# Embedding stage of a hybrid decoder step: row factor applied in the gate's tanh, norm weights folded into the gate's weights, the affine step folded into the products, and the last tile's input projection issued ahead

## The chip, the core and the metric

The kernel runs on one core of a Trainium2 chip. The core has five engines that run side by side and wait for each other by semaphores: TensorE (PE in the profile, with its weight loads as PEld), VectorE (DVE), ScalarE (ACT), GpSimd (POOL) and SyncE (SP). Each engine works through its own instructions in the order that was fixed when the kernel was built. Transfers are issued from the queues of SP, ACT and POOL and carried by 16 DMA engines. The metric is the time of one execution on the device, in microseconds (us). Times of the same kernel in several runs are given by their median.

## What is computed

One layer of a decoder: RMSNorm and token mixing (retention and RWKV-7), a mixture of experts with product keys (PEER), then the per-layer input embedding that the change is about, and a final RMSNorm. There are 1024 prompt tokens and 64 sample tokens, the model is 1024 wide, and an input row has 256 elements. Cut to the end of the layer:

```python
def rmsnorm(x, g):
    y = x * lax.rsqrt(jnp.mean(x * x, axis=-1, keepdims=True) + RMS_EPS)
    return y * g
...
    h = h + peer(rmsnorm(h, norm_ffn), peer_wq, peer_keys, peer_u, peer_v)
    gate = jax.nn.sigmoid(rmsnorm(h, ple_norm) @ ple_gate)
    h = h + gate * (p_l @ ple_proj)
...
    y = rmsnorm(h, norm_final)
```

The row factor of a norm is 1/sqrt(mean + eps), one number for each token. `g`, here `ple_norm`, is one number for each of the 1024 columns.

## The kernel before

**Tokens and tiles.** The 1088 tokens are nine tiles: 0 to 7 with 128 prompt tokens each, and tile 8 with the 64 sample tokens. The mixture of experts is computed in two ways. For tiles 0 and 1 (`E0`) and tiles 8, 2 and 3 (`G1`) the chosen rows of the two expert tables are gathered: `gather` fetches, for each of a token's 128 experts, one row of 4 KB per token by an indirect DMA on POOL's queue (L1157, 128 rows of 4 KB in one fetch, into one of five buffers named `grow`). VectorE makes the dot product with it (L1171, first table) or adds it, weighted, to the running sum `gacc` (L1185, second table). For tiles 4 to 7 (`G2`) all 16384 experts are computed with matmuls: `dense_fused` and `dense_stored` call `dense`, which loads a piece of the second table (`vraw`, four buffers), splits it, and adds to `yT`.

**Splitting.** fp32 operands are split in a high and a low part (`split`, L304 to L308): ScalarE copies and rounds the high part, and VectorE (L306) or GpSimd (L308) subtracts it. `mm3` (L333 to L336) then makes three matmuls: high by high, high by low, low by high.

**The embedding stage's weights.** `ple_weights` runs as a side task within `dense_stored`, one step at every fourth piece of the table. Each step loads 128x512 of a weight into one of the `vraw` buffers (tile `pgr`, L1420) and splits it on ScalarE and GpSimd: 4 pieces for the projection (`pproj`), 16 for the gate (`pgate`). The parts lie in `pga`, `pgb` and `pgx`.

**The embedding stage.** `ple` (L1424 on) goes through the tiles in the order 0, 1, 4, 5, 6, 7, 8, 2, 3. It takes small tiles from one of two pools in turn, and `h` from three buffers. For each tile it

- loads the tile's input rows, transposed (`pt`, L1433), and splits them into `pth` and `ptl`, the low part on VectorE;
- loads h (L1438) and adds the experts' result: for tile 3, the last, the gather's sum straight from its PSUM home (L1440); for the other gathered tiles from DRAM (`py`, L1444, L1445); for tiles 4 to 7 transposed out of `yT` (`pyt`, L1450, L1451);
- calls `norm_T` (L310 on): Square with a sum on ScalarE (L314, `njunk`), the root on GpSimd in two instructions (`rsq`, L298, L299, `nrs`), then on VectorE h times row factor times `ple_norm` (L318, also into `njunk`), and `split_T`: eight transposes on TensorE (L327, `ntr`) and the split into `pxh` and `pxl`;
- for each half of 512 columns: 24 matmuls of the gate (`ppg`), tanh on ScalarE (L1460, `psg`), `0.5 t + 0.5` on VectorE (L1461, which makes the sigmoid), 6 matmuls of the input projection (`ppp`), product (L1464) and addition to h (L1465). `ppg` and `ppp` come from the same two PSUM buffers;
- for the final norm: Square (L1468, `fsq`), root (`frs`), two products (L1473, `fin`), and two stores from ACT's queue (L1474).

The gather of tile 3 is issued in the text ahead of `dense`, and it still runs while the first eight tiles go through `ple`. The last tile's h therefore waits for the last of its 128 sums.

**What sets the order.** The kernel is written with a framework that fixes each engine's order at build time: a list scheduler takes, on a modelled timeline, the ready instruction that stands first in the program text. It is switched on by `tile.TileContext(nc, schedule_with_timeline_sim=True)`. So an edit to one instruction can move others on every engine. Tiles of one pool with the same tag share buffers, and the next user of a buffer waits until the last reader is done.

## Time and profile before

| | us |
|---|---|
| runs shown: lowest, median, highest (3) | 3652.43, 3653.45, 3653.52 |
| profiled execution, its own time | 3657.16 |
| profiled execution, span from first to last instruction | 3655.2 |
| PE busy | 3242.7 (89%) |
| DVE busy | 2842.8 (78%) |
| POOL busy | 2343.4 (64%) |
| ACT busy | 1215.9 (33%) |

The profile is one execution on the chip, recorded by the hardware. A row of a *group* gives line, engine and operation, result and operands by their names in the program with their shapes, the count, the busy time and the mean duration in ns, and behind the second bar the idle time of that engine just before, with what ended most of it. A row of the *timeline* gives start, duration, engine, line, operation, and in brackets the idle time before. A row of a *window* table gives, for one stretch, its length, the busy time (and number of instructions) of each engine, the clock granted to TensorE as a share of full speed, the share of time in which the DMA engines were busy, and the GB/s that they moved. A row of *waits* gives who waited for whom, the sum, the number of times and the longest.

### The profile page before, as it was taken

To read this page: it belongs to the slowest core of one execution; us is meant where nothing else is said; L and a number is where in the kernel's file an instruction comes from. 1 tells how busy PE (TensorE), PEld (TensorE's weight loads), DVE (VectorE), ACT (ScalarE), POOL (GpSimd) and SP (SyncE) were. 2 spreads that over 40 slices of the span, in tenths; PEclk is the share of its full clock that TensorE was granted. 3 is DMA by queue.
4 is the path that set the end of the run, shared out by engine and by line. 5 is a ranking of instruction groups with operands and counts; after the bars stand their busy time and mean duration, and the time that the engine had idled before them with its cause. 6 is when DMAs were issued, how large, how long until landed. Compare 5 with 4: busy or idle time off the path is not lost. (4 is left out here: it accounts for less than half of the span.)

```text
span 3655.2 us, 51715 instructions
## 1 busy us (share of the span) xinstructions
PE 3242.7 (89%) x17493; PEld 2685.5 (73%) x17493; DVE 2842.8 (78%) x5663; ACT 1215.9 (33%) x2247; POOL 2343.4 (64%) x2076
## 2 busy tenths in 40 slices
PE   7797996887878888879999999899999999889995
PEld 7697996764756666758877887788888877667773
DVE  4544688888797787879977999777777777788887
ACT  4233121111211111222235888843333333333321
POOL 5352677554445555544489786578888878888743
PEclk9798997557978777889999999999999999999997
DMA  7267599779957888896589988899999999999975
GB/s 263 89 198 237 196 328 325 258 275 312 323 191 266 295 277 282 283 345 211 170 268 328 349 296 331 321 315 340 339 349 342 344 325 371 360 369 365 328 249 186
DMA packets 416995, 1059.97 MB, mean 290 GB/s; under 512 B 45467, under 2 KB 140953, under 8 KB 412058
## 3 DMA queue, kind: packets, MB, share of 16 engines
q0 software_dynamic: 165888, 604.05, 46.3%
q1 hardware_dynamic: 197902, 364.96, 30.1%
q10 hardware_dynamic: 52940, 87.64, 6.4%
q8 instruction: 139, 2.28, 0.2%
q14 instruction: 126, 1.03, 0.1%
HBM read 968.88 MB, written 87.56 MB: 289 GB/s over the span
## 5 line engine op out<-in xcount | busy, mean ns | idle before, releaser
L1157 POOL DMA_INDIRECT grow<-in_pv,eid x576 | 568.6, 987 | 500.7 <-DVE gacc L1185 244.9
L1157 POOL DMA_INDIRECT grow<-in_pu,eid x576 | 562.3, 976 | 355.3 <-DVE grow L1171 209.6
L1185 DVE SCALAR_TENSOR_TENSOR gacc<-grow,ac,gacc 128x1024 f32<-128x1024 f32 x571 | 731.6, 1281 | 49.7 <-DMA grow<-in_pv,eid 41.9
L1171 DVE SCALAR_TENSOR_TENSOR grow<-grow,gacc 128x1024 f32<-128x1024 f32 x576 | 689.5, 1213 | 83.0 <-DMA grow<-in_pu,eid 76.7
L1347 PE MATMUL py<-ah,vh 128*128 128x512 f32 x1024 | 405.0, 396 | 28.2 <-ACT vh L304 25.6
L333 PE MATMUL ph<-cx,uh 128*128 128x512 f32 x1024 | 404.1, 395 | 3.3 <-ACT uh L304 3.2
L1348 PE MATMUL py<-al,vh 128*128 128x512 f32 x1024 | 403.8, 394 | 0.5 <-DVE al L306 0.5
L334 PE MATMUL ph<-cx,uh 128*128 128x512 f32 x1024 | 402.2, 393 | 0.0
L308 POOL TENSOR_TENSOR vl<-vraw,vh 128x512 fp32r<-128x512 f32 (+2 forms) x232 | 327.5, 1416 | 31.1 <-ACT vh L304 19.9
L308 POOL TENSOR_TENSOR ul<-uraw,uh 128x1024 fp32r<-128x1024 f32 x128 | 308.2, 2408 | 50.4 <-ACT uh L304 30.3
L1350 PE MATMUL py<-ah,vl 128*128 128x512 f32 x1024 | 276.0, 398 | 16.2 <-POOL vl L308 15.7
L336 PE MATMUL ph<-cx,ul 128*128 128x512 f32 x1024 | 265.0, 395 | 3.9 <-POOL ul L308 3.9
L1347 PEld LDWEIGHTS py<-ah,vh 128*128 128x128 f32 x1024 | 194.3, 190 | 78.8 <-ACT vh L304 34.5
L304 ACT ACTIVATE vh<-vraw 128x512 fp32r<-128x512 f32 (+2 forms) x232 | 156.1, 675 | 280.0 <-PE py L1348 99.0
L1350 PEld LDWEIGHTS py<-ah,vl 128*128 128x128 f32 x1024 | 190.7, 189 | 70.8 <-POOL vl L308 30.8
L1354 DVE TENSOR_TENSOR yT<-yT,py 128x512 f32<-128x512 f32 x224 | 153.1, 684 | 109.0 <-PE py L1350 99.7
L1348 PEld LDWEIGHTS py<-al,vh 128*128 128x128 f32 x1024 | 194.5, 190 | 42.6 <-DVE al L306 1.9
L333 PEld LDWEIGHTS ph<-cx,uh 128*128 128x128 f32 x1024 | 192.8, 188 | 42.6 <-ACT uh L304 4.1
L336 PEld LDWEIGHTS ph<-cx,ul 128*128 128x128 f32 x1024 | 191.4, 189 | 43.4 <-POOL ul L308 5.4
L334 PEld LDWEIGHTS ph<-cx,uh 128*128 128x128 f32 x1024 | 193.0, 188 | 38.1
L304 ACT ACTIVATE uh<-uraw 128x1024 fp32r<-128x1024 f32 x128 | 135.5, 1059 | 169.9 <-DMA uraw<-in_puT 96.1
L1296 PEld LDWEIGHTS pwt<-oh 128*128 128x128 f32 x1024 | 143.4, 201 | 47.8 <-ACT wst L1297 19.1
(403 smaller groups left out, 7198.0 us busy)
## 6 DMA issues: line engine op xcount, KB each, us to landing
uraw<-in_puT SPq DMA_DIRECT2D x128, 512.0 KB
vraw<-in_pvd SPq DMA_DIRECT2D x112, 320.0 KB
cw<-in_w_out SPq DMA_DIRECT2D x128, 256.0 KB
wd<-wst ACTq DMA_DIRECT2D x28, 1024.0 KB
wt<-wd SPq DMA_DIRECT2D x64, 448.0 KB
vraw<-in_pvd SPq DMA_DIRECT2D x112, 256.0 KB
wraw<-in_w_ret SPq DMA_DIRECT2D x48, 512.0 KB
wraw<-in_w_rw SPq DMA_DIRECT2D x42, 512.0 KB
```

The source lines that it names most:

```text
L304: nc.scalar.activation(hi, src, AF.Copy)
L308: nc.gpsimd.tensor_tensor(lo, src, hi.bitcast(F32), op=OP.subtract)
L333: mm(out, lh(k), rh(k), start=first and k == 0, stop=False)
L334: mm(out, *((ll(k), rh(k)) if right else (lh(k), rl(k))), start=False, stop=False)
L336: mm(out, *((lh(k), rl(k)) if right else (ll(k), rh(k))), start=False, stop=last and k == nk - 1)
L1157: nc.gpsimd.indirect_dma_start(out=g, out_offset=None, in_=src, in_offset=bass.IndirectOffsetOnAxis(ap=self.eid[t][:, j:j + 1], axis=0))
L1171: nc.vector.scalar_tensor_tensor(g[:, c], g[:, c], 1.0, x[:, c], op0=OP.mult, op1=OP.mult, accum_out=hv[:, i, j:j + 1])
L1185: nc.vector.scalar_tensor_tensor(y[:, c], g[:, c], ac[:, j:j + 1], y[:, c], op0=OP.mult, op1=OP.add)
L1347: nc.tensor.matmul(p, vh[:, b, :], ah, start=b == 0, stop=False)
L1348: nc.tensor.matmul(p, vh[:, b, :], al, start=False, stop=False)
L1350: nc.tensor.matmul(p, vl[:, b, :], ah, start=False, stop=b == nb - 1)
L1354: nc.vector.tensor_tensor(yT[:, d, :], yT[:, d, :], p, op=OP.add)
```

## The change

The formulas say the same thing in another order. With s the row factor and g the norm's weights, (h s g) W is s (h (g W)), so g can go into the gate's weights once and s, one number per row, can be applied after the matmul. The sigmoid is 0.5 + 0.5 tanh(x/2), so the tanh gets s/2 as its scale (`rsq` is called with 4/D and 4e-6, which gives half the root), and the `+1` and the `0.5` go into the two VectorE instructions that stood behind it: (tanh + 1) times projection, then 0.5 times that plus h.

- `norm_T` is replaced: Square and root stay, the row product (L318) goes, and `split_T` transposes h itself.
- The norm's row, loaded to all partitions (L245, `row_ple_norm`), is no longer loaded. The norm's weights come as 128x8 columns (`pn`), and each of the 16 gate pieces is multiplied by its column on ScalarE, in place, before it is split.
- The affine step (L1461) goes; product and addition become `scalar_tensor_tensor`.
- The low part of `pt` is subtracted on GpSimd instead of VectorE.
- For tile 3 both halves of the input projection are written in the text ahead of the gate's matmuls, into the two-bank buffer that tiles 4 to 7 use for `pyt`.

```diff
+    r['pnorm'] = f(i['ple_norm'])[0].reshape(8, 128).T
...
+        self.pn = rp.tile([128, 8], F32, name="pnorm")
...
+        nc.sync.dma_start(self.pn, I['pnorm'])
...
                     nc.sync.dma_start(raw, I[src][k, :, cs])
+                    if src == 'pgate':
+                        nc.scalar.activation(raw, raw, AF.Copy, scale=self.pn[:, k:k + 1])
                     self.split(w[0][k][:, cs], w[1][k][:, cs], raw, "g")
...
-        gr, gf = self.row(tps[0], 'ple_norm'), self.row(tps[1], 'norm_final')
+        gf = self.row(tps[1], 'norm_final')
...
-            self.split(pth[:, :, :n], ptl[:, :, :n], pt[:, :, :n])
+            self.split(pth[:, :, :n], ptl[:, :, :n], pt[:, :, :n], "g")
...
-            self.norm_T(tp, h, n, gr, xh, xl, 0)
+            njunk = tp.tile([128, D], F32, name="njunk")
+            nss = tp.tile([128, 1], F32, name="nssq")
+            nc.scalar.activation(njunk[:n], h[:n], AF.Square, accum_out=nss[:n])
+            hr = self.rsq(tp, nss, n, 4.0 / D, 4e-6, 1, "nrs")
+            self.split_T(h, n, xh, xl, 0)
+            ahead = []
+            if t == G1[-1]:
+                q = self.pst.tile([128, 2, 512], F32, name="pyt")
+                for c in range(2):
+                    ahead.append(q[:, c])
+                    self.mm3(q[:n, c], lambda k: pth[:, k, :n], lambda k: ptl[:, k, :n], lambda k: ph[k][:, c * 512:c * 512 + 512], lambda k: pl[k][:, c * 512:c * 512 + 512], 2)
             for c in range(2):
...
-                nc.scalar.activation(sg[:n], p[:n], AF.Tanh, scale=0.5)
-                nc.vector.tensor_scalar(sg[:n], sg[:n], 0.5, 0.5, op0=OP.mult, op1=OP.add)
-                p2 = self.ps("ppp", "p")
-                self.mm3(p2[:n], lambda k: pth[:, k, :n], lambda k: ptl[:, k, :n], lambda k: ph[k][:, cs], lambda k: pl[k][:, cs], 2)
-                nc.vector.tensor_tensor(sg[:n], sg[:n], p2[:n], op=OP.mult)
-                nc.vector.tensor_tensor(h[:n, cs], h[:n, cs], sg[:n], op=OP.add)
+                nc.scalar.activation(sg[:n], p[:n], AF.Tanh, scale=hr[:n])
+                p2 = ahead[c] if ahead else self.ps("ppp", "p")
+                if not ahead:
+                    self.mm3(p2[:n], lambda k: pth[:, k, :n], lambda k: ptl[:, k, :n], lambda k: ph[k][:, cs], lambda k: pl[k][:, cs], 2)
+                nc.vector.scalar_tensor_tensor(sg[:n], sg[:n], 1.0, p2[:n], op0=OP.add, op1=OP.mult)
+                nc.vector.scalar_tensor_tensor(h[:n, cs], sg[:n], 0.5, h[:n, cs], op0=OP.mult, op1=OP.add)
```

## The prediction

> **What bounds the kernel now.** I read the page's span first, then a table of windows over the last 190 us, because all that is edited apart from the weight preparation runs there, then the groups of instructions of that stage by engine, the waits of TensorE, and last the timeline of the final 32 us, row by row.
>
> ```profile
> span 3655.2 us, 51715 instructions
> ```
>
> ```profile
> core 0: us, PE busy (x) PEld busy (x) DVE busy (x) ACT busy (x) POOL busy (x), PEclk, DMA share, GB/s
> 3465.00:3600.00 135.00, 122.41 (x561) 95.29 (x559) 122.25 (x151) 36.16 (x68) 69.61 (x77) 0.98 0.77 258
> 3600.00:3624.00 24.00, 0.00 (x0) 0.00 (x0) 20.26 (x17) 0.00 (x0) 11.47 (x12) 0.50 0.83 293
> 3624.00:3655.00 31.00, 17.20 (x68) 13.40 (x68) 9.00 (x13) 4.69 (x8) 1.49 (x4) 0.78 0.05 17
> ```
>
> The columns are the stretch, its length, and the busy time of each engine. The embedding stage falls into three parts. **Part one**, 3465 to 3600: eight of the nine tiles pass through it while the expert gather of the last tile (tile 3) runs beside them. TensorE and VectorE are each busy for 122 of 135 us, so neither is far from being the limit. **Part two**, 3600 to 3624: TensorE does nothing at all; only the gather's last rows are summed. **Part three**, 3624 to the end: tile 3 alone, one dependent chain with no other work beside it. What is saved in part three is saved in full. What is saved in part one counts only if the gather's sums end earlier.
>
> ```profile
> L1185 DVE SCALAR_TENSOR_TENSOR gacc<-grow,ac,gacc 128x1024 f32<-128x1024 f32 x16 | 20.6, 1289 | 3.4 <-DMA grow<-in_pv,eid 3.0
> ```
>
> This is the group of the gather's sums from 3598.3 to 3624.2: 16 of them in about 25.8 us, so **1.61 us per row left over** after the tiles are through. They wait for DMA, so a freer VectorE makes them no faster; only their number counts. The order of instructions on each engine is fixed when the kernel is built, from a modelled timeline, so this number is a matter of order.
>
> **The change, part by part. (a) The last tile's chain.**
>
> ```profile
> 3624.12 1.22 DVE L1440 TENSOR_TENSOR ph<-ph,gacc 128x1024 f32<-128x1024 f32 x1
> 3625.38 1.06 ACT L314 ACTIVATE njunk<-ph 128x1024 f32<-128x1024 f32 x1 [25.70 <-DVE ph L1440]
> 3626.89 0.56 POOL L299 TENSOR_TENSOR nrs<-nrs,halves 128x1 f32<-128x1 f32 x1
> 3627.49 1.28 DVE L318 SCALAR_TENSOR_TENSOR njunk<-ph,nrs,row_ple_norm 128x1024 f32<-128x1024 f32 x1 [2.14 <-POOL nrs L299]
> 3628.92 1.94 PE L327 MATMUL ntr<-csta,njunk 128*128 128x128 f32 x8 [33.80 <-DVE njunk L318]
> ...
> 3633.57 0.40 PE L333 MATMUL ppp<-pgb,pth 128*128 128x512 f32 x1
> ...
> 3634.96 0.40 PE L333 MATMUL ppg<-pgb,pxh 128*128 128x512 f32 x1
> ...
> 3639.53 0.50 PE L333 MATMUL ppg<-pga,pxh 128*128 128x512 f32 x1 [0.69 <-ACT psg L1460]
> ...
> 3645.43 0.60 ACT L1460 ACTIVATE psg<-ppg 128x512 f32<-128x512 f32 x1 [5.95 <-PE ppg L336]
> ...
> 3646.07 0.43 DVE L1461 TENSOR_SCALAR psg<-psg 128x512 f32<-128x512 f32 x1 [4.61 <-ACT psg L1460]
> ...
> 3646.84 0.69 DVE L1464 TENSOR_TENSOR psg<-psg,ppp 128x512 f32<-128x512 f32 x1 [0.35 <-PE ppp L336]
> 3647.57 0.69 DVE L1465 TENSOR_TENSOR ph<-ph,psg 128x512 f32<-128x512 f32 x1
> ```
>
> The columns are start, duration, engine, line, and in brackets the idle time before. Four pieces go.
>
> First, the transposes now read h itself. They waited for Square, the root on GpSimd and the row product, which ends at 3627.49 + 1.28 = 3628.77; now they wait only for the sum that ends at 3624.12 + 1.22 = 3625.34. That is **3.43 us**. Square stays and now runs beside the transposes; it and its reading of the sum are over about 1.2 us after the addition, as before, and the first hi copy of the transposed tile falls due on the same engine 3630.04 - 3628.92 = 1.12 us after the transposes start. The two just miss each other, so I cost it at nothing; if they met, some 0.1 us would be lost.
>
> Second, the projection `ppp` of the first half stood between two blocks of the gate's matmuls: 3634.96 - 3633.57 = **1.39 us**. It depends on pt only, and the last of the nine low parts of pt was made at 3582.8 (row below), so it can run in the empty part two; its buffer is the one that the last G2 tile leaves.
>
> ```profile
> L306 DVE TENSOR_TENSOR ptl<-pt,pth x9: 279/418/427, 3437.2 to 3582.8; 128x256 fp32r<-128x256 f32 x8, 128x128 fp32r<-128x128 f32 x1
> ```
>
>
> Third, the second half's gate waited 0.69 us for the first tanh to give its PSUM buffer back; with the projection in another pool the second buffer is free: **0.69 us**, with nothing for the slow first matmul.
>
> Fourth, behind the last tanh the affine step goes and the wait for the second projection with it: the product started at 3646.84 and can start at 3646.07, **0.77 us**. The two VectorE instructions left become scalar_tensor_tensor with constants. This trace has that form at the same length as a plain addition: 1.21 us in the first row below against 1.22 at L1440, so nothing is added.
>
> ```profile
> L1171 DVE SCALAR_TENSOR_TENSOR grow<-grow,gacc 128x1024 f32<-128x1024 f32 x576 | 689.5, 1213 | 83.0 <-DMA grow<-in_pu,eid 76.7 <-issue 3.0 <-ACT wst L1297 1.8
> L755 ACT ACTIVATE th<-pa,kah x36: 307/368/378, 139.3 to 1491.1; 128x128 f32<-128x128 f32 x32, 128x64 f32<-128x64 f32 x4
> L1239 ACT ACTIVATE es<-epq x32: 257/278/278, 335.3 to 1024.6; 128x128 f32<-128x128 f32 x32
> ```
>
> The tanh takes its factor from a column of SBUF now. The nearest pair of rows is a 128x128 tanh with such a column (median 368 ns) and a copy of the same size from PSUM without one (278): 0.09 us more, once on the path. Part (a) is -(3.43 + 1.39 + 0.69 + 0.77) + 0.09 = **-6.2 us**, and I see no cover that could hide it, since nothing else runs there.
>
> **(b) VectorE in part one.**
>
> ```profile
> L1185 DVE SCALAR_TENSOR_TENSOR gacc<-grow,ac,gacc 128x1024 f32<-128x1024 f32 x50 | 63.9, 1279 | 0.5 <-DMA grow<-in_pv,eid 0.4
> ...
> L318 DVE SCALAR_TENSOR_TENSOR njunk<-ph,nrs,row_ple_norm 128x1024 f32<-128x1024 f32 (+1 forms) x7 | 9.0, 1279 | 0.5 <-POOL nrs L299 0.5
> L1461 DVE TENSOR_SCALAR psg<-psg 128x512 f32<-128x512 f32 (+1 forms) x16 | 6.7, 418 | 1.0 <-ACT psg L1460 1.0
> ...
> L306 DVE TENSOR_TENSOR ptl<-pt,pth 128x256 fp32r<-128x256 f32 (+1 forms) x8 | 3.2, 400 | 0.0
> ```
>
> From 3465 to 3600, VectorE loses 9.0 + 6.7 + 3.2 = 18.9 us of 122.25. Then TensorE is the limit, and it loses nothing.
>
> ```profile
> 3465.00:3594.90 129.90, 122.19 (x561) 95.29 (x559) 117.18 (x146) 35.01 (x66) 66.58 (x74) 0.99 0.76 254
> ```
>
> ```profile
> PE ppg L333 <- ACT psg L1460: 5.5, 2, 4.1
> ```
>
> Until its last matmul before the gap (3594.9) TensorE is idle for 129.90 - 122.19 = 7.7 us, 5.5 of it in two waits for a tanh that gives a PSUM buffer back. So the gain lies between 0 and 7.7 us. I take about half, **-4**: the tanh's own tile and the next one's norm lie in the chain that the change shortens, but a tile's h is still loaded only when the third tile before it is finished.
>
> **(c) The order that follows.** 50 sums lie among eight tiles, 6.25 per tile. If the model behind the order sees the tiles pass sooner, it places fewer sums among them and leaves more to part two, 1.61 us each. At the 4 of 133 us of (b) that is 1.5 rows: **+2**. From the other side, VectorE's new room could let it place three more ahead: -5. If the model is bound by VectorE alone, up to 18.9/133 = 14%, 7 rows, go behind: +11.
>
> **(d) Work put on other engines.**
>
> ```profile
> L304 ACT ACTIVATE pga<-pgr 128x512 fp32r<-128x512 f32 x8 | 5.0, 623 | 2.4 <-DMA pgr<-in_pgate 2.3
> ```
>
> ```profile
> PE py L1347 <- ACT vh L304: 25.6, 18, 3.7
> ```
>
> ```profile
> ACT vh L304 <- DMA vraw<-in_pvd: 55.9, 26, 6.4
> ```
>
> Sixteen pieces of the gate's weights get one more ScalarE instruction each, 0.62 + 0.09 = 0.71 us, in the dense stage. Behind it in ScalarE's queue stand the hi copies of the expert weights, for which TensorE waited 18 times (2980 to 3465), and those copies mostly waited for their DMA. All sixteen in front of such a copy would cost 11.4 us; none costs nothing. The copies' own waits were for DMA (55.9 us in 26 waits from 3055 to 3315), and a scaling that runs inside such a wait delays nobody, so I stay near the lower end: **+0.5**.
>
> ```profile
> L308 POOL TENSOR_TENSOR vl<-vraw,vh 128x256 fp32r<-128x256 f32 x8 | 5.9, 748 | 2.0 <-issue 1.9
> ```
>
> ```profile
> L1157 POOL DMA_INDIRECT grow<-in_pv,eid x48 | 55.8, 1163 | 43.0 <-DVE gacc L1185 36.7 <-issue 2.6 <-DVE ph L1465 1.6
> ```
>
> The subtraction for pt's low part goes to GpSimd at 0.75 us, 8 times in part one: 6 us. Row fetches queue behind it there, but GpSimd idles 43 us before them, 36.7 waiting for sums to free buffers: **0**. If that cover went, it would be 6. The load of the norm's columns is 4 KB on SP's queue, well ahead: 0.
>
> **(e) The norm row's load.**
>
> ```profile
> 3423.38 0.38 SPq L245 DMA_DIRECT2D row_ple_norm<-in_rows  x1
> ```
>
> ```profile
> 3423.00:3443.00 20.00, 16.98 (x75) 13.66 (x73) 13.71 (x17) 4.47 (x8) 12.84 (x12) 1.00 0.96 356
> ```
>
> ```profile
> 3443.69 0.50 PE L1347 MATMUL py<-ah,vh 128*128 128x512 f32 x1 [3.70 <-ACT vh L304]
> ...
> 3444.97 0.59 PE L1348 MATMUL py<-al,vh 128*128 128x512 f32 x1
> ...
> 3448.85 0.39 PE L1347 MATMUL py<-ah,vh 128*128 128x512 f32 x1
> ```
>
> The 512 KB row goes out on SP's queue ahead of the expert weights whose late arrival stops TensorE for 3.70 us; at 356 GB/s it takes 1.5 us. It is gone: **-1.5**, between 0 and the whole stall, -3.7.
>
> ```profile
> 3238.97 0.50 PE L1347 MATMUL py<-ah,vh 128*128 128x512 f32 x1 [2.39 <-ACT vh L304]
> ...
> 3240.26 0.63 PE L1348 MATMUL py<-al,vh 128*128 128x512 f32 x1
> ```
>
> After the 3.70 us gap ten matmuls took 3448.85 - 3444.97 = 3.9 us instead of some 2.3 (six in 1.39 us in (a)). The Trainium skill ("TensorE: Matmul & The Clock Gate", Part 1) says that the clock halves after an idle window of about 3.4 us; by it the gap shortened to 2.2 us keeps the clock, and (e) would be -3.1. The trace disagrees: a gap of 2.39 us at 3238.97 was followed by 0.63 us matmuls too. So I stay with -1.5.
>
> **The sum** is -6.2 - 4 + 2 + 0.5 - 1.5 = -9.2 us. The profiled execution took 3657.16 us, 2.0 more than its span, so it would take 3648.0; the median of the three runs is 3.7 us lower, 3653.45, and the forecast for it is **3644.2 us**. About 0.2%, 7.3 us, is what a measurement of this kernel can tell from no change: below 3646.1 is faster, above 3660.8 slower.
>
> **The rivals.** *Only the end counts.* TensorE's 7.7 us stay, since the loads of h set them, and the order does not move: -6.2 - 1.5 + 0.5, 3646.2. For it: three h buffers and an 80% busy DMA. Against it: VectorE's 122 of 135 us. *More ahead.* The order puts three more sums among the tiles and TensorE closes its gaps: -6.2 - 7.7 - 5 - 1.5 + 0.5, 3633.5. *Given back in the dense stage.* Ten of the sixteen scalings meet a waiting copy, +7: 3651. Against it: those copies wait for DMA. *Slower: the order moves against the gather.* Place: VectorE's order from 3465 to 3600. Price: 1.61 us for each sum that falls behind the tiles. The rest of the sum is -11.2, so it decides from 7 rows on; at 12 rows it is +8.1, 3661.6. For it: fewer instructions of the tiles in the model. Against it: 7 rows is all that VectorE's relief can give if the model is bound by it, and more needs the shorter chain too.
>
> **How the numbers follow.** The forecast 0.45, more ahead 0.12, only the end 0.20, given back 0.08, order against 0.15. Faster by over 0.2%: most of the first, all of the second and an edge of the third, 0.56. Slower: half of the last, 0.08. The rest, 0.36, is within 0.2%. The range leaves out the far end of "more ahead" and of "order against": 3635 to 3655.
>
> **What would show it.** (a): tile 3's transposes start 0.1 us after the addition, no `ppp` lies after it, and from the addition's start to the span's end it is 24.9 us, not 31.1. (b): TensorE idles under 4 us in part one. (c): the count of sums after the last tile before tile 3 is 16 to 19; over 22 and the forecast is wrong. (d): TensorE's wait for the hi copies stays near 25.6 us. (e): the stall at 3440 is near 2 us.

## Result, and the profile after

| | before | after |
|---|---|---|
| median of nine runs each on one chip (us) | 3655.25 | 3633.83 |
| lowest and highest (us) | 3650.61, 3669.21 | 3618.93, 3643.74 |
| ratio, with its 95% interval | 1 | 0.9946 (0.9929 to 0.9964) |
| span of the profiled execution (us) | 3655.2 | 3632.1 |

The change makes the kernel 0.54% faster, about 20 us (13 to 26 by the interval). The forecast was 9.2 us, less than half of that.

Below, "the stage" is the stretch from the first gate product (`ppg`) to the start of tile 3's addition of the gather's sum, and "the chain" is the stretch from there to the span's end. In the two profiles the stage falls from 159.3 to 145.4 us and the chain from 31.1 to 25.0.

First the windows of the kernel before: the eight tiles (up to the last addition to h ahead of tile 3), and what of the gather comes after them.

```profile
core 0: us, PE busy (x) PEld busy (x) DVE busy (x) ACT busy (x) POOL busy (x), PEclk, DMA share, GB/s
3464.80:3597.76 132.96, 122.61 (x563) 95.49 (x561) 120.24 (x149) 35.07 (x67) 68.37 (x76) 0.99 0.77 257
3597.76:3624.12 26.36, 0.00 (x0) 0.00 (x0) 22.56 (x20) 1.15 (x2) 12.80 (x14) 0.52 0.83 294
```

The same two windows of the kernel after:

```profile
3461.69:3600.02 138.33, 128.05 (x575) 100.92 (x573) 120.16 (x130) 36.28 (x67) 78.30 (x96) 0.96 0.85 290
3600.02:3607.10 7.08, 0.00 (x0) 0.00 (x0) 6.97 (x8) 1.15 (x2) 0.74 (x2) 0.69 0.62 242
```

The eight tiles themselves did not get shorter: 138.3 us against 133.0, 2.7 of it tile 3's twelve input products, which now run among them. VectorE is busy for the same 120 us beside them. But it does other work in that time: the wait behind the tiles has shrunk from 26.4 to 7.1 us. The timeline of VectorE shows why. Before (the last row is tile 3's, behind the addition):

```profile
3603.99 3.94 DVE L1185 SCALAR_TENSOR_TENSOR gacc<-grow,ac,gacc 128x1024 f32<-128x1024 f32 x3
3609.70 7.93 DVE L1185 SCALAR_TENSOR_TENSOR gacc<-grow,ac,gacc 128x1024 f32<-128x1024 f32 x6 [1.77 <-DMA grow<-in_pv,eid]
3617.92 1.29 DVE L1185 SCALAR_TENSOR_TENSOR gacc<-grow,ac,gacc 128x1024 f32<-128x1024 f32 x1 [0.29 <-DMA grow<-in_pv,eid]
3620.15 3.94 DVE L1185 SCALAR_TENSOR_TENSOR gacc<-grow,ac,gacc 128x1024 f32<-128x1024 f32 x3 [0.93 <-DMA grow<-in_pv,eid]
...
3630.67 0.69 DVE L306 TENSOR_TENSOR pxl<-ntr,pxh 128x512 fp32r<-128x512 f32 x1 [1.90 <-ACT pxh L304]
```

After:

```profile
3600.02 0.68 DVE L1480 SCALAR_TENSOR_TENSOR ph<-psg,ph 128x512 f32<-128x512 f32 x1
3600.62 2.61 DVE L1187 SCALAR_TENSOR_TENSOR gacc<-grow,ac,gacc 128x1024 f32<-128x1024 f32 x2
3603.13 1.41 DVE L1488 SCALAR_TENSOR_TENSOR fin<-ph,frs,row_norm_final 128x512 f32<-128x512 f32 x2
3604.46 2.61 DVE L1187 SCALAR_TENSOR_TENSOR gacc<-grow,ac,gacc 128x1024 f32<-128x1024 f32 x2
3607.10 1.22 DVE L1445 TENSOR_TENSOR ph<-ph,gacc 128x1024 f32<-128x1024 f32 x1
3610.22 0.69 DVE L308 TENSOR_TENSOR pxl<-ntr,pxh 128x512 fp32r<-128x512 f32 x1 [1.90 <-ACT pxh L306]
```

The columns are start, duration, engine, line, operation with its count, and in brackets the idle time before. Before, 13 sums of the gather stand behind the eighth tile's final scaling (16 behind its last addition to h); after, 2 (and 4). VectorE's order is fixed when the kernel is built, so this is a count in the program and no accident of a run: the time that the removed work took on VectorE among the tiles has been filled with twelve more sums of the gather. (The groups that were removed add up to 18.9 us. VectorE's busy time in the stage falls by 15.7, mostly because an instruction starts some 0.08 us before the end of the one ahead of it, as the rows above show.)

The last row shows the other gain. The low part of tile 3's transposed h is due 3.1 us after the addition starts, and was due 6.6 us after it, with the norm's product in between.

### The profile page after: what moved, and what is told of

Same layout as the page of the kernel before. It is cut to its first block, busy times and chain, and to the rows that moved or that the text cites. A ratio compares the mean times of both kernels' runs of the same rounds, so it can differ in the third digit from the quotient of the medians.

```text
span 3632.1 us, 51684 instructions
## 1 busy us (share of the span) xinstructions
PE 3237.5 (89%) x17493; PEld 2676.3 (74%) x17493; DVE 2821.9 (78%) x5627; ACT 1226.5 (34%) x2263; POOL 2339.5 (64%) x2085
## 5 line engine op out<-in xcount | busy, mean ns | idle before, releaser
L1349 PE MATMUL py<-ah,vh 128*128 128x512 f32 x1024 | 402.7, 394 | 31.8 <-ACT vh L306 27.5
L310 POOL TENSOR_TENSOR ul<-uraw,uh 128x1024 fp32r<-128x1024 f32 x128 | 307.9, 2405 | 54.0 <-ACT uh L306 28.6
L1298 PEld LDWEIGHTS pwt<-oh 128*128 128x128 f32 x1024 | 145.9, 205 | 50.1 <-ACT oh L1295 21.7
```

What stands on the lines that cost most here:

```text
L310: nc.gpsimd.tensor_tensor(lo, src, hi.bitcast(F32), op=OP.subtract)
L1349: nc.tensor.matmul(p, vh[:, b, :], ah, start=b == 0, stop=False)
```

## The experiments

Three theories were to be told apart. **A**: the time hangs on how many sums the order leaves behind the tiles, 1.61 us each. **B**: the shorter chains and the fewer operations shorten the tiles themselves, and the order is beside the point. **C**, formed after the first four runs: in the stage VectorE's work is the bound, and what is taken from it comes off the stage nearly whole.

All thirteen kernels in one table. Each ratio is to the kernel before in the same session; "sums" counts those that start behind the eighth tile's last addition to h; "profile only" stands where there is one profiled execution and no ratio. In the two kernels marked "-" an addition to h stands behind tile 3's own, so the count means something else.

| kernel | sums | stage, us | VectorE busy in it, us | chain, us | ratio to before (95% interval) |
|---|---|---|---|---|---|
| before | 16 | 159.3 | 142.8 | 31.1 | 1 |
| before, second profile | 16 | 163.5 | 142.7 | 30.7 | - |
| after | 4 | 145.4 | 127.1 | 25.0 | 0.9946 (0.9929 to 0.9964) |
| after, order undone | 16 | 163.3 | 128.3 | 24.4 | 0.9993 (0.9974 to 1.0012) |
| before, order of after | 9 | 163.7 | 142.0 | 31.5 | 0.9997 (0.9983 to 1.0011) |
| after, a row product put back | 10 | 158.8 | 134.5 | 24.9 | 0.9974 (0.9958 to 0.9990) |
| after, nothing done ahead | 6 | 144.2 | 127.0 | 28.6 | 0.9954 (0.9931 to 0.9977) |
| before, only the fold | 11 | 153.9 | 133.8 | 29.3 | 0.9998 (0.9977 to 1.0019) |
| before, only no affine step | 13 | 155.7 | 138.0 | 30.8 | 0.9986 (0.9965 to 1.0007) |
| before, only done ahead | 14 | 159.3 | 142.7 | 28.4 | profile only |
| after, norm row loaded | 4 | 144.1 | 127.3 | 25.3 | profile only |
| after, final scaling moved | - | 140.0 | 120.4 | 26.4 | 0.9946 (0.9918 to 0.9974) |
| after, TensorE kept busy | 4 | 145.4 | 127.1 | 23.6 | 0.9946 (0.9924 to 0.9968) |
| both of these | - | 141.0 | 122.2 | 24.7 | 0.9928 (0.9902 to 0.9953) |

### The kernel before, profiled again

The kernel unaltered.

> The kernel before, unaltered, profiled a second time, to learn how well one profile tells the lengths that the comparisons rest on. If the order of the instructions fixes them: 159.3 us from the first gate product to tile 3's addition, within 2, and 31.1 us from there to the span's end, within 0.5, while the start of the stage may lie elsewhere by 20 us, as in the profiles so far. If they are chance, the stage differs by 5 us or more and the comparisons of single profiles fall.

The chain came back within 0.4 us, the stage 4.2 us longer (163.5 against 159.3). That is more than the 2 us expected and less than the 5 that would make single profiles useless: a difference of a stage under some 4 us is not read below, one of 14 is, and one of 5 to 8 is a hint that needs others beside it. The times of one kernel spread by about 1% from run to run, and most of that lies ahead of the stage, whose start lay anywhere from 3442 to 3465 us; so the parts are compared by stage and chain, and the ratios only checked against them.

### The order undone, and the order alone

The steps of tile 3's gather run where they did but for the last 16, whose sums are queued on VectorE behind tile 2's last fused addition (`self.done`).

```diff
+ HELD = 16
...
+ for _ in range(256 - HELD): next(steps)
+ self.held = steps
...
  if t == G1[-1]:
+     with self.tc.issue_after(self.done.ins):
+         for _ in self.held: pass
      nc.vector.tensor_tensor(h[:n], h[:n], self.sums, op=OP.add)
```

> The changed kernel with its own work and one thing undone: the order. The last sums of tile 3's gather are queued on VectorE behind tile 2's last fused add, so that 13 of them stand behind the eighth tile, as in the kernel before, and not 2. Theory A (the number of sums left behind the tiles sets when the gather ends): the sums end 15 to 18 us later than 3607.1 (11 sums at 1.61 us, less up to 2.3 us by which the tiles end earlier with fewer sums among them), the chain from tile 3's addition to the span's end stays 25.0 us, and the time is 15 to 18 us above the changed kernel's, level with the kernel before less the 6.1 us of the chain. Theory B (the operations removed shorten the tiles themselves and the order is beside the point): the tiles end as much earlier as sums are taken out of them, the gather ends within 5 us of 3607.1, and the time is within 5 us of the changed kernel's.

The stage is 163.3 us, 17.9 longer than after, and the kernel is level with the kernel before (0.9993), although its chain is the short one. Theory A's range was 15 to 18; theory B falls. Where the work of these sums is missing from the tiles, they don't end earlier:

```profile
core 0: us, PE busy (x) PEld busy (x) DVE busy (x) ACT busy (x) POOL busy (x), PEclk, DMA share, GB/s
3445.97:3582.37 136.40, 127.02 (x575) 99.67 (x573) 105.76 (x118) 36.35 (x67) 68.46 (x85) 0.97 0.77 261
3582.37:3609.29 26.92, 0.00 (x0) 0.00 (x0) 22.57 (x20) 1.15 (x2) 11.78 (x13) 0.58 0.68 234
```

VectorE works 14.4 us less beside the tiles (105.8 against 120.2), and they take 136.4 us against 138.3. So with the change made, the tiles last as long as TensorE's 127 us and its waits, and VectorE has room beside them. Then the reverse, the kernel before with the order of after (`self.gi` holds tile 3's sums, `BACK` the one that each tile's final scaling is queued behind):

```diff
+ BACK = [-54, -46, -40, -33, -26, -18, -12, -3]
...
- nc.vector.scalar_tensor_tensor(fin[:n], h[:n, cs], r[:n], gf[:n, cs], op0=OP.mult, op1=OP.mult)
+ with (self.tc.issue_after(self.gi[BACK[i]].ins) if i < 8 else ExitStack()):
+     nc.vector.scalar_tensor_tensor(fin[:n], h[:n, cs], r[:n], gf[:n, cs], op0=OP.mult, op1=OP.mult)
```

> The kernel before with all its work, and VectorE's order forced: the final scalings of each of the eight tiles are queued behind as many sums as in the changed kernel, so that 2 sums stand behind the tiles and not 13. Theory A in its plain form (order alone): the sums end 15 to 18 us earlier than 3624.1 and the time is 13 to 18 us under the kernel before, with the chain behind tile 3's addition still 31.1 us. Theory A with room (the sums need the VectorE time that the change frees): from 3465 to 3600 VectorE is busy 122.3 of 135 us in the kernel before, 12.7 us are free and eleven sums take 14.1, so that the tiles end later by what doesn't fit; then each sum that is moved gains only 1.61 less 1.28 us, 3.6 us for all eleven, and the time is 2 to 8 us under the kernel before. Theory B: no change, within 2 us.

```profile
core 0: us, PE busy (x) PEld busy (x) DVE busy (x) ACT busy (x) POOL busy (x), PEclk, DMA share, GB/s
3453.99:3601.98 147.99, 125.88 (x563) 97.50 (x561) 128.54 (x156) 35.46 (x67) 72.98 (x83) 0.95 0.77 257
3601.98:3617.65 15.67, 0.00 (x0) 0.00 (x0) 13.42 (x13) 1.15 (x2) 5.75 (x7) 0.54 0.75 248
```

The wait behind the tiles falls from 26.4 to 15.7 us, and the tiles grow from 133.0 to 148.0. The stage is 163.7 us, no shorter than in the two profiles of the kernel before, and the time the same (0.9997), which is also what theory B expected. The plain form of theory A falls with it: **here the order alone, without the freed time on VectorE, was worth nothing.** "A with room" expected 2 to 8 us, and even that was too much. Part of the loss is the experiment's own. VectorE now waits for h among the tiles:

```profile
DVE ph L1454 <- DMA ph<-hd: 9.6, 3, 5.4
DVE ph L1448 <- DMA ph<-hd: 4.8, 2, 3.5
```

These are 14.4 us, against 7.6 in the kernel before. A scaling that is queued later gives its h buffer back later, and that would explain it, but it wasn't tested by itself. It can't hide much: all of VectorE's idle time in the stage is 21.7 us, against 16.5 and 20.9 in the two profiles of the kernel before, so without the edit's own waiting the stage would be shorter by some 1 to 5 us (an estimate from these three), not by the 13 to 18 of theory A.

### A row product put back

```diff
  self.split_T(h, n, xh, xl, 0)
+ dj = tp.tile([128, D], F32, name="njunk")
+ nc.vector.scalar_tensor_tensor(dj[:n], h[:n], 1.0, h[:n], op0=OP.mult, op1=OP.mult)
```

> The changed kernel with a VectorE product of a whole row for each tile put back (1.28 us, as the norm's product was), whose result nothing reads, so that it delays no chain by itself; with it 7 sums stand behind the eighth tile and not 2. Theory A: five more sums at 1.61 us, the gather ends 6 to 9 us later and the time is 6 to 9 us above the changed kernel's, with the chain behind tile 3's addition at 25 to 26.3 us (the product of tile 3 itself lies beside the transposes). Theory B: the product is off every chain and costs under 2 us.

The stage grew by 13.4 us and the chain not at all; the ratio went half of the way back, to 0.9974. Theory B falls again. The size is above theory A's 6 to 9 us. By VectorE's work alone it should be 7.4 us (134.5 against 127.1). The rest is idle time that the experiment itself brought, as the groups of VectorE in the stage show (the product, the additions of the experts' result to h, and the gather's sums):

```profile
L1465 DVE SCALAR_TENSOR_TENSOR njunk<-ph 128x1024 f32<-128x1024 f32 (+1 forms) x7 | 8.6, 1222 | 3.1 <-ACT njunk L1461 3.1
L1456 DVE TENSOR_TENSOR ph<-ph,pyt 128x1024 f32<-128x1024 f32 x4 | 4.9, 1220 | 11.2 <-DMA ph<-hd 11.2
L1450 DVE TENSOR_TENSOR ph<-ph,py 128x1024 f32<-128x1024 f32 (+1 forms) x4 | 4.9, 1216 | 2.6 <-DMA ph<-hd 2.2 <-DMA py<-yd 0.4
L1187 DVE SCALAR_TENSOR_TENSOR gacc<-grow,ac,gacc 128x1024 f32<-128x1024 f32 x64 | 82.2, 1284 | 4.6 <-DMA grow<-in_pv,eid 3.9
```

The product's tile shares its buffer with Square's scratch, so VectorE stood 3.1 us waiting for ScalarE. VectorE stood 4.6 us ahead of the sums, mostly for their rows, against 2.1 in the kernel after. The two additions stood 13.8 us between them, as in the kernel after (13.5, below): these waits have only moved from one to the other. It isn't a clean measure of 1.28 us per tile; that it costs, and not B's 2 us, is clear.

### The parts one by one

Only the fold, with the scaled weights and without the load of the norm's row as in the change, but with the affine step, `ptl` on VectorE and nothing done ahead:

```diff
- self.norm_T(tp, h, n, gr, xh, xl, 0)
+ nc.scalar.activation(njunk[:n], h[:n], AF.Square, accum_out=nss[:n])
+ hr = self.rsq(tp, nss, n, 4.0 / D, 4e-6, 1, "nrs")
+ self.split_T(h, n, xh, xl, 0)
...
+ nc.scalar.activation(sg[:n], p[:n], AF.Tanh, scale=hr[:n])
```

> One part of the change alone: the norm folded into the gate (row factor in the tanh, weights scaled), with the affine step, the subtraction of the inputs' lower parts on VectorE and the place of the last projection all as before. It takes 1.28 us of VectorE work per tile away, 10.2 in all, and the order leaves 8 sums behind the eighth tile and not 13. Theory C, formed from the first runs (between the first gate product and tile 3's addition VectorE is the bound, so that what is taken from it comes off nearly whole: 15.7 us fewer gave 13.9): that stage falls from 159.3 us by 7 to 10, the chain behind it from 31.1 by 3.4 to 27.7, and the time is 10 to 14 us under the kernel before. Theory A by count: five sums at 1.61 us, 8.0, and 3.4: 11.5 us under. Theory B: 3.4 us under.

Only the affine step taken out:

```diff
- nc.vector.tensor_scalar(sg[:n], sg[:n], 0.5, 0.5, op0=OP.mult, op1=OP.add)
- nc.vector.tensor_tensor(sg[:n], sg[:n], p2[:n], op=OP.mult)
- nc.vector.tensor_tensor(h[:n, cs], h[:n, cs], sg[:n], op=OP.add)
+ nc.vector.scalar_tensor_tensor(sg[:n], sg[:n], 1.0, p2[:n], op0=OP.add, op1=OP.mult)
+ nc.vector.scalar_tensor_tensor(h[:n, cs], sg[:n], 0.5, h[:n, cs], op0=OP.mult, op1=OP.add)
```

> The other part of the VectorE work alone: the kernel before with its norm and everything else, but without the affine step (two instructions of 0.42 us per tile, 6.7 us from 3465 to 3600), its two constants taken into the two following instructions. 10 sums stand behind the eighth tile and not 13. Theory C: the stage falls from 159.3 us by 4 to 7, as VectorE's work does, and the chain behind it from 31.1 by up to 0.8. Theory A by count: three sums at 1.61 us, 4.8, and as much of the chain. Theory B: only the chain, under 1 us. The time is 4 to 8 us under the kernel before by the first two.

Only the last tile's projection of inputs done ahead:

```diff
+ if t == G1[-1]:
+     q = self.pst.tile([128, 2, 512], F32, name="pyt")
+     for c in range(2):
+         ahead.append(q[:, c])
+         self.mm3(q[:n, c], ...)
```

> The kernel before with only the last tile's projection of inputs done ahead. The chain behind tile 3's addition falls from 31.1 by 1.4 to 2.1 us, to 29.0 to 29.7. VectorE's work is as before; 11 sums stand behind the eighth tile and not 13. Theory C: the stage stays at 159.3 us within 2.5, since nothing is taken from VectorE. Theory A by count: it falls by 3.2 us.

Against the mean of the two profiles of before (stage 161.4, chain 30.9): the fold takes 9.0 us less work on VectorE and shortens the stage by 7.5; without the affine step it is 4.8 us less work and 5.7 us; the projection done ahead takes nothing from VectorE and leaves the stage at 159.3, inside the two profiles. The two shortenings make 13.2 of the 16.0 us of the whole change. That is what theory C expects; A's counts (8.0, 4.8 and 3.2 us) fit the first two as well, and the third not well. For chains, the projection done ahead was worth 2.4 us by itself, the fold 1.6, no affine step nothing that can be read.

Measured from the first profile, as the expectations were, it looks worse for theory C: the fold's stage fell by 5.4 us and not 7 to 10, and the stage without the affine step by 3.6 and not 4 to 7. Both fit only against the mean of the two profiles. The fold's chain fell to 29.3, not to 27.7. So these two runs support theory C, with differences not far above the spread; they don't prove it alone.

The timed ratios are less kind still. Without the affine step it is 0.9986, and its interval reaches 1. For the fold it is 0.9998 where 10 to 14 us were expected, and where stage and chain give 9.1 us, 0.25%. That is just outside the interval (0.9977 at its lower end), so something ahead of the stage cost a few us there. Most of it is found below, under (d).

The whole change without the projection done ahead:

```diff
- if t == G1[-1]:
+ if False:
      q = self.pst.tile([128, 2, 512], F32, name="pyt")
```

> The changed kernel without the last tile's projection of inputs done ahead: its two products come behind the gate's again. Both theories: the chain from tile 3's addition to the end grows from 25.0 by 1.39 us (the products of the second half) and up to 0.7 us (PSUM buffer), to 26.4 to 27.1 us. Theory A adds 1.6 us, because 3 sums stand behind the eighth tile and not 2: 3 to 4 us above the changed kernel's time. Theory B: 1.4 to 2.1 us above it.

The chain is 28.6 us, 3.7 longer and not 1.4 to 2.1: the products of both halves and the wait for the PSUM buffer (0.84 us) count. The stage, with three of the sums behind the scaling and not two, is 144.2 us, no longer than after. One row of A's price can't be told from none.

### The norm row's load

```diff
- gf = self.row(tps[1], 'norm_final')
+ gr, gf = self.row(tps[0], 'ple_norm'), self.row(tps[1], 'norm_final')
```

> The changed kernel with the load of the gate norm's weights for all partitions kept (512 KB, as in the kernel before, read by nobody); the order of VectorE is the changed kernel's. If the load is what held TensorE up before the first gate product of the stage in the kernel before (a stall of 3.7 us at 3443.7, and 23.4 of 25 us busy from 3440 in the changed kernel), the stall is there again and TensorE is idle some 1.5 us longer in the 25 us before the stage's first gate product. If the load costs nothing, that stretch is as in the changed kernel. The stage behind it is 145.4 us to within 2 in both cases.

The stall is back. The timeline of TensorE:

```profile
3433.14 1.32 PE L1352 MATMUL py<-ah,vl 128*128 128x512 f32 x5
3437.93 0.80 PE L1349 MATMUL py<-ah,vh 128*128 128x512 f32 x1 [3.47 <-ACT vh L306]
...
3441.94 0.63 PE L1350 MATMUL py<-al,vh 128*128 128x512 f32 x1
3442.37 2.14 PE L1352 MATMUL py<-ah,vl 128*128 128x512 f32 x5
3444.35 0.40 PE L1349 MATMUL py<-ah,vh 128*128 128x512 f32 x1
```

The five products took 1.32 us ahead of the stall and 2.14 behind it. What it costs altogether is seen in VectorE's additions to `yT`, whose order is the same in both kernels. With the load:

```profile
3434.50 0.69 DVE L1356 TENSOR_TENSOR yT<-yT,py 128x512 f32<-128x512 f32 x1 [1.64 <-PE py L1352]
3444.55 0.69 DVE L1356 TENSOR_TENSOR yT<-yT,py 128x512 f32<-128x512 f32 x1 [6.84 <-PE py L1352]
```

The same two additions in the kernel after:

```profile
3442.04 0.69 DVE L1356 TENSOR_TENSOR yT<-yT,py 128x512 f32<-128x512 f32 x1 [2.79 <-PE py L1352]
3445.48 0.69 DVE L1356 TENSOR_TENSOR yT<-yT,py 128x512 f32<-128x512 f32 x1 [0.22 <-PE py L1352]
```

10.05 us against 3.44: the load costs 6.6 us at this place, 3.5 in the stall and the rest in products at half the granted clock behind it. The five profiles with the load and the rest of the kernel before around it show a stall there too, of 2.36 to 3.70 us, and the eight without the load none above 0.63. So the mechanism of the load is shown; its price in the kernel before wasn't measured by itself. An estimate comes from the last stretch ahead of the first gate product (from the 992nd product with a low part of the expert weights on): 26.8 to 29.8 us in the five with the load, 24.7 in each of the eight without, 31.2 with the load put back.

### More work off VectorE

```diff
+ if t == G1[-1]:
      nc.vector.scalar_tensor_tensor(fin[:n], h[:n, cs], r[:n], gf[:n, cs], op0=OP.mult, op1=OP.mult)
+ else:
+     nc.scalar.activation(fin[:n], h[:n, cs], AF.Copy, scale=r[:n])
+     nc.gpsimd.tensor_tensor(fin[:n], fin[:n], gf[:n, cs], op=OP.mult)
```

> The changed kernel with one more piece taken off VectorE: the final scaling of the eight tiles ahead of tile 3 (two products of 0.71 us each, 1.4 us a tile) is done by ScalarE (row factor) and GpSimd (norm weights); tile 3's stays on VectorE. Theory C: VectorE has some 10 us less to do between the first gate product and tile 3's addition; the stage falls from 145.4 us by 5 to 9, until TensorE's own 128 us and its waits bind it, and the time is 5 to 9 us under the changed kernel's. Rival (the changed kernel's stage is bound by TensorE or by the rows that the gather fetches): under 2 us gained. Second rival (GpSimd, which also starts the gather's fetches in order, is now late with them, each product there at 1.3 us or more): the stage grows by up to 10 us.

The stage fell by another 5.4 us to 140.0, within C's 5 to 9, so after the change VectorE is still the bound, though TensorE is close. VectorE's busy time fell by 6.7 us only and not by 10. The two timelines, VectorE's and GpSimd's, tell why:

```profile
3571.90 1.28 DVE L1187 SCALAR_TENSOR_TENSOR gacc<-grow,ac,gacc 128x1024 f32<-128x1024 f32 x1
3573.09 3.00 DVE L1480 SCALAR_TENSOR_TENSOR ph<-psg,ph 128x512 f32<-128x512 f32 x1
```

```profile
3573.00 2.54 POOL L1492 TENSOR_TENSOR fin<-fin,row_norm_final 64x512 f32<-64x512 f32 x2
```

The addition to h, 0.68 us by itself, took 3.00 beside the two products of GpSimd; two others took 1.51 and 1.77, which makes 4.2 us for the three. The chain grew by 1.4 us to 26.4. Of this, 0.9 is tile 2's Square, which now stands on ScalarE ahead of tile 3's copies; the rest is that nine of tile 3's products ran at half rate and not six. Stage and chain together make it 4.0 us better than after; the ratio is the same 0.9946 with a wider interval, which can't show that.

### TensorE kept busy in the gap, and both together

The added products are queued behind tile 2's last product (`self.last`) and come ahead of tile 3's transposes.

```diff
+ if t == G1[-1]:
+     wm = self.ps("warm", "p")
+     with self.tc.issue_after(self.last):
+         for k in range(44):
+             nc.tensor.matmul(wm, wh[0][:, :128], wh[0][:, :512], start=True, stop=True)
```

> The changed kernel with 44 matmuls that nothing reads put on TensorE between tile 2's last product and tile 3's transposes, where it sits idle for 10.6 us at present. Theory (the granted clock, 0.50 from 3607 to 3611 and 0.69 to 3614 behind that idle time, is what makes the first twelve of tile 3's gate products take 0.43 us apart and not 0.23, and the transposes 1.9 us): with TensorE kept busy the chain from tile 3's addition to the span's end falls from 25.0 to between 22.5 and 23.5 us, all else equal, so 1.5 to 2.5 us under the changed kernel's time. Rival (what slows them is not the idle time, but the wait for their operands): the chain stays at 25.0 us. If the matmuls run past the addition, up to 1 us is lost again.

The order of VectorE is that of the kernel after, and the stage came out the same to 0.1 us (145.4). The chain fell to 23.6, just above the 22.5 to 23.5 expected. The first products of tile 3 in the kernel after:

```profile
3608.47 1.94 PE L329 MATMUL ntr<-csta,ph 128*128 128x128 f32 x8 [10.60 <-DVE ph L1445]
3610.24 0.79 PE L335 MATMUL ppg<-pga,pxh 128*128 128x512 f32 x1
3610.83 0.63 PE L336 MATMUL ppg<-pga,pxh 128*128 128x512 f32 x1
```

With TensorE kept busy:

```profile
3582.82 10.13 PE L1475 MATMUL warm<-pga 128*128 128x512 f32 x44
3594.54 1.07 PE L329 MATMUL ntr<-csta,ph 128*128 128x128 f32 x8 [1.59 <-DVE ph L1446]
3596.11 0.50 PE L335 MATMUL ppg<-pga,pxh 128*128 128x512 f32 x1 [0.51 <-ACT pxh L306]
3596.45 0.40 PE L336 MATMUL ppg<-pga,pxh 128*128 128x512 f32 x1
```

Eight transposes in 1.07 us and not 1.94, and the products at 0.40 at once. The rival (operands) falls: ScalarE's first copy starts only 0.2 us sooner after the addition (2.31 us and not 2.49), the first product even waits 0.51 us for it, and the chain is 1.4 us shorter all the same. (The expectation speaks of twelve slow products in the kernel after; the profile has six, up to 3612.54.) The two that helped, together:

> The two that helped put together: the changed kernel with the final scaling of the first eight tiles on ScalarE and GpSimd, and 14 unread matmuls in TensorE's gap of 3.7 us before tile 3's transposes. The stage is 140 us as it was with the scaling moved, the chain behind it falls from 26.4 to between 24.5 and 25.5 us, and the time is 5 to 7 us under the changed kernel's, 0.6 to 0.8% under the kernel before. If the gap is too short to have lowered the granted clock, the chain stays at 26.4 us and the gain at 4 us.

The diff is that of the last two, with 14 matmuls for 44. The stage is 141.0 us and the chain 24.7, as expected, and the ratio 0.9928 (0.9902 to 0.9953) the best of all: some 26 us under the kernel before. By stage and chain it is 4.7 us better than after; the intervals of the two overlap, so the measured times don't show that it is better than the change.

## Why the prediction was right, and where not

The sign was right. The measured ratio, 0.9946, lies just past the lower end of the range (3635 is 0.9950), which its interval still holds. The size forecast was less than half of what came, and the step on the order, (c), had the wrong sign. Point by point:

**(a) The chain, -6.2: the sum was right, its parts less so.** 25.0 us from the addition to the end, against the 24.9 named and 31.1 before. In the kernel with the fold alone the first gate product starts 3.14 us after the addition, before 6.57: the 3.43 us of the sum to the digit. That these 3.43 are worth only 1.6 there is mostly the clock: ten products ran at half rate there, and five and three in the two profiles of the kernel before. Between 3 and 10 were slow in the kernels without the added products, at some 0.2 us each, which alone makes single chains differ by up to 1.4 us; an early start doesn't decide it (three with the order undone, ten with the fold). So that the whole chain came out within 0.1 us is in part luck. The tanh with its factor from a column took 0.69 us against 0.60, the 0.09 expected. The projection done ahead is worth more than its two terms (1.39 + 0.69) say: 3.7 us with the rest of the change in. In the kernel without it the first half's products take 1.43 us between the gate's, the wait for the PSUM buffer 0.84, and 0.78 lie between the last tanh and the product that waits for the second half's. The prediction had the last of these in its fourth piece, under the affine step, whose removal alone brought nothing.

**(b) The tiles, -4: wrong in form.** TensorE was to idle under 4 us in part one; it idles 138.33 - 128.05 = 10.3 in the window above, 2.2 of it behind its last product, so 8.1 where it was 7.7. The tiles end no earlier, with or without the sums among them (138.3 and 136.4 us). What VectorE was relieved of didn't shorten the tiles at all.

**(c) The order, +2: this step failed, in sign and size.** It named 16 to 19 sums after the last tile; there were 4. The step took the order to hold a given number of sums per tile, so that tiles passing sooner would leave more behind. The order rather fills VectorE's free time: 15.7 us of its busy time in the stage were freed, and twelve more sums went in among the tiles, 14.4 us (120.2 with them, 105.8 where the order is undone). The 5 us that the step allowed for "three more ahead" had no derivation; dividing the freed time by the length of a sum would have given up to 14. With (b) the prediction had -2 us for the stage; it fell by 13.9 between the first two profiles, 16.0 against the mean of both profiles of before. The observation that a freer VectorE makes the sums left over no faster, and that their number counts, was right, and so is the reading of part two as empty time. Wrong was "neither is far from being the limit" as the end of the matter: two engines with 122 of 135 us each, and 16 sums still outstanding, meant that work taken off VectorE could be replaced at once.

The rival "more ahead" has the mechanism, and 3633.5 lies beside what was measured, but by a wrong sum: 7.7 us from TensorE's idle time, which stayed, and 5 for sums in place of 14 to 16.

The pattern that the runs leave: in eleven of the fourteen profiles, the stage is VectorE's busy time in it plus 16.5 to 20.9 us, a spread as wide as that of the two profiles of the kernel before. The exceptions are the order undone (35.0), the product put back (24.2) and the order forced on the kernel before (21.7), in which the edit itself made VectorE wait. So the gain of the stage needs both: the freed time, and an order that puts the sums into it.

**(d) Scaling on ScalarE, +0.5: not settled.** From the dense stage's first product to the first gate product took 1040.5 to 1049.4 us in the five profiles without the scaling and 1042.9 to 1053.3 in the eight with it and without the row load; the means are 1042.6 and 1047.1. None of these 4.5 us lies where the scalings run: from the 512th to the 864th product with a low part of the expert weights, the stretch that holds all sixteen, it is 284.0 us without and 283.7 with them in the mean (282.4 to 286.8, and 278.6 to 289.1). That is no proof of 0.5; it speaks against the rival's +7. The wait of TensorE for the high parts, 25.6 us before and 27.5 after, can't tell: it is 19.7 to 25.6 in the five and 23.5 to 32.5 in the eight.

The 4.5 us are a sum of things that the prediction didn't have. Some 2 are lost before the first scaling (below, without a cause). About 3.8 are gained in the last stretch, where the load of the norm's row is gone. And 5.5 to 7.1 are lost just ahead of that, from the 864th to the 992nd of these products, in every kernel with the scaled weights and in none without. Before and after (rows of windows, without their heading), and TensorE's waits in them:

```profile
3345.55:3435.01 89.46, 89.08 (x389) 72.60 (x388) 71.76 (x97) 33.89 (x54) 70.60 (x58) 1.00 0.98 352
PE py L1347 <- ACT vh L304: 0.4, 1, 0.4
```

```profile
3342.00:3436.97 94.97, 90.30 (x389) 72.50 (x388) 75.28 (x100) 33.88 (x56) 71.94 (x59) 1.00 0.96 346
PE py L1349 <- ACT vh L306: 2.8, 2, 1.4
PE py L1350 <- DVE al L308: 1.7, 1, 1.7
```

The last scaling is done by then. In the wait for `al` a sum of the gather stands on VectorE just ahead of the split that TensorE waits for. VectorE's order differs from the one before here too, this time against the kernel. It also answers most of the question that the fold left open: the fold alone loses 5.5 us here, and 3.4 ahead of the stage in all. With its 9.1 us of stage and chain that leaves 5.7 us, 0.16%, which the interval of its ratio holds. Which line of the edit moves the order wasn't tested.

**(e) The row's load, -1.5: right mechanism, too small.** The load's 512 KB at 356 GB/s are 1.5 us of transfer, but what counts is the stall that they start and the slow products behind it: 6.6 us in the kernel after, above the "whole stall, -3.7" named as the far end, and by the estimate above 2.1 to 5.1 us in the kernel before. "The stall near 2 us" was wrong as well: without the load there is none above 0.63.

The prediction did well not to let the length of the stall decide the clock. Behind the stalls of 3.70, 3.24, 2.56 and 3.47 us nine or more products ran at half rate. Behind one of 3.44 us (the order forced on the kernel before) and one of 2.36 (only no affine step) none did. And in six of the nine kernels with the scaled weights eight or more did so behind the wait of 1.65 us for `al`. The Trainium skill ("TensorE: Matmul & The Clock Gate", Part 1) has the clock halve after an idle window of about 3.4 us; for the length of a single gap these traces don't bear that out, in either direction. The -3.1 that the prediction weighed by it and left is nearer to what the load cost.

Together: stage -13.9 to -16.0, chain -5.7 to -6.1, ahead of the stage some +4.5 in the mean, with single profiles 9 to 10 us apart. That is about 15 to 18 us, and 20 (13 to 26) were measured.

## What to carry to other kernels

Where a planner fixes the order and some work waits for whatever time is left, count that work as part of the engine's load: here the stage got shorter where VectorE had less to do in all and the order put the waiting sums into the freed time. Neither the freed time without that order (163.3 us) nor that order without the freed time (163.7 us) shortened it. And look for what the new order does elsewhere: it cost 5.5 us or more ahead of the stage. Before costing an edit by "that engine isn't the bound here", ask what will be put in its place, and divide the freed time by its length. For the next step, look at what VectorE waits for, here mostly h (the kernel after):

```profile
L1456 DVE TENSOR_TENSOR ph<-ph,pyt 128x1024 f32<-128x1024 f32 x4 | 4.9, 1219 | 6.5 <-DMA ph<-hd 6.5
L1450 DVE TENSOR_TENSOR ph<-ph,py 128x1024 f32<-128x1024 f32 (+1 forms) x4 | 4.9, 1219 | 7.0 <-DMA ph<-hd 4.4 <-DMA py<-yd 2.7
```

13.5 of some 18 us in which VectorE is idle in the stage of the kernel after are spent ahead of these additions; a fourth buffer for h was not tried.

## What the hardware showed beside that

**An addition that shares its way with GpSimd.** The addition to h (both operands in SBUF) takes 0.68 us. With the final scaling moved, four of them ran at the same time as a product of GpSimd: 1.51, 1.77 and 3.00 us, and 0.69 where the two shared only 0.27 us. With both edits together it was 1.51 and 2.98, and 0.68 and 0.69 in two short meetings. The sums of the gather, which read the running sum in PSUM, kept to 1.27 to 1.29 us in all 27 meetings of these two kernels. In the kernel after one such addition was stretched to 1.21 us beside the subtraction of `ptl`, which was itself stretched:

```profile
3519.54 1.21 DVE L1480 SCALAR_TENSOR_TENSOR ph<-psg,ph 128x512 f32<-128x512 f32 x1
```

```profile
3520.13 1.21 POOL L310 TENSOR_TENSOR ptl<-pt,pth 128x256 fp32r<-128x256 f32 x1
3535.08 0.75 POOL L310 TENSOR_TENSOR ptl<-pt,pth 128x256 fp32r<-128x256 f32 x1
```

The Trainium skill ("GPSIMD Engine Reference", 1. Specifications) says that GpSimd's interfaces to SBUF are shared with VectorE, with contention from VectorE instructions that have two SBUF inputs; the trace agrees, and the gather's sums, with one of their inputs in PSUM, are spared. The prediction had cost the move of `ptl` at nothing and asked only whether fetches queue behind it. This one meeting added 0.5 us to VectorE's work; the other subtractions met no such addition.

**How long the half clock lasts.** From the transposes' start to the end of the last slow product it took 3.3 to 6.8 us in the profiles of kernels without the added products, and one slow product was left with them. The Trainium skill ("TensorE: Matmul & The Clock Gate", Part 1) has activity watched in windows of some 3.4 us that run freely, so that the step depends on where the first product falls. A spread agrees with that, but this one, 3.5 us wide, is larger than the 0.5 us either way that the page gives.

**2.1 us without a cause.** The 80th addition to `yT` of the dense stage starts 433.6 us after the first product there in all nine profiles with the scaled weights, and 431.5 us after it in the five without. The scaling comes 200 us later, and the load of the norm's columns is long done (issued at 17 us). One group of products is a little longer in each instance there, 391 against 389 ns in the mean; its row from the kernel after, and from the kernel before:

```profile
L335 PE MATMUL ph<-cx,uh 128*128 128x512 f32 x316 | 123.7, 391 | 0.0
```

```profile
L333 PE MATMUL ph<-cx,uh 128*128 128x512 f32 x316 | 122.9, 389 | 0.0
```

That is 0.8 of the 2.1 us. The cause wasn't found.
